# A hybrid attention, Fourier and MLP layer on eight cores: transposed layout, folded DFT, norms applied at evacuation, instruction order computed by list scheduling

## The chip, the cores and the metric

One Trainium2 chip, eight cores, one program on all of them. Each batch entry is shared by two cores: a core owns 1,024 of the 2,048 tokens and computes keys, values and Fourier inputs for all 2,048, so no core talks to another. The metric is the device time of the slowest core in microseconds (us). Some executions fall into a slower state in which the cores of one die show a lower granted clock.

Some words: PSUM is the memory that TensorE writes its sums to, in banks, and an evacuation is the instruction that reads them out; a slot is a buffer for a block of weights; a transfer lands when its data are there; the chain is the work that ended last, followed back from the end of the program to what each step waited for.

## The reference, cut to what matters

```python
h = modulate(rmsnorm(x, g1), sh1, sc1)        # x (4, 2048, 2048); h*(1+scale)+shift
q, k, v, u = split_proj(h @ w_in)             # 1536 | 512 | 512 | 512 columns
q = apply_axial_rope(rmsnorm(heads(q, 12), q_g), tabs)
k = apply_axial_rope(rmsnorm(heads(k, 4), k_g), tabs)
attn = latent_attention(q, k, v, kc, vc)      # keys: 2048 latent + 256 context tokens
four = fourier_mix(u, w_f)                    # Re(2-D DFT over tokens and channels), then a 128x128 map
x = x + gt1 * (concat([attn, four]) @ w_out)
h2 = modulate(rmsnorm(x, g2), sh2, sc2)
x = x + gt2 * (square(relu(h2 @ w1)) @ w2)    # 2048 -> 8192 -> 2048
return rmsnorm(x, final_norm_g)
# the six shifts, scales and gates: silu(c) @ w_ada + b_ada, w_ada being 2048 x 12288
```

All weights come as fp32 and are turned into bf16 by the load.

## The kernel before

Tokens lie on the partitions. x is normalised, transposed 128 by 128 on TensorE, and scale and shift are applied as the transpose is copied out. The modulation comes first, eight blocks, because the shift is needed at that copy:

```python
for j in range(8):
    ada_block(j, 0, 1)                        # shift1 and scale1, 8 x 4.19 MB, all before any norm
...
groups = [(x_oth[0:512, :], 4, 0, 'gs0', 0, [3, 4, 5], 1024, 1024), ...]   # five token groups
...
            for cb in blocks:                 # w_in is fetched again for each of the five groups
                s = wb_next()
                wv = WB[s].rearrange("p (k n) -> p k n", k=16)
                dma('pool', wv, w_in[:, cb * 512:(cb + 1) * 512].rearrange("(k p) n -> p k n", p=128), ...)
                for t in range(ntiles):
                    ...
```

Attention works on halves of a head (512 queries), 24 in all, over 18 chunks of 128 keys. Half of the softmax denominator is summed on TensorE and half on VectorE:

```python
        NPT = 4                               # buffers of exponentials
...
            mm(PS(ob), Vt[:, ch, kh * 128:(kh + 1) * 128], PT[p], ch == 0, ch == 17, ...)
            if ch % 2 == 1:
                mm(PS(ob + 1), ones_bf, PT[p], ch == 1, False, ...)
            elif ch == 0:
                S.add('dve', lambda e, da=da, p=p: e.tensor_copy(out=DACC[da], in_=PT[p]), ...)
            else:
                S.add('dve', lambda e, da=da, p=p: e.tensor_tensor(out=DACC[da], in0=DACC[da], in1=PT[p], op=ALU.add), ...)
...
                S.add('dve', lambda e, rd=rd, ob=ob: e.reciprocal(out=RDEN[rd], in_=PS(ob + 1)), ...)
```

Then come the Fourier groups, 272 matmuls of 512 columns; the output projection, whose weights use the slots of the modulation blocks; a second norm with transposes; sixteen MLP blocks of 256 matmuls; and a final norm, row by row. Each engine runs the order in which the program names the operations.

## Time and profile before

Three executions took 2,193.15 to 2,196.6 us, median 2,195.57.

| of the profiled execution | value |
|---|---|
| busy share: TensorE, VectorE, ScalarE, GpSimd | 83, 43, 29, 18% |
| instructions | 29,071 |
| transposes on TensorE | 584 |
| HBM read | 386.61 MB, of it w_in 84 MB (20 blocks of 4.19 MB) |
| modulation and first norm | 0 to 190 us |
| projections of K, V, U and Q | 190 to 597 us |
| attention | 626 to 1,043 us |
| Fourier, output projection | 1,043 to 1,095, 1,125 to 1,277 us |
| MLP, final norm | 1,277 to 2,163, 2,163 to 2,196 us |

Read 83% as an average over two different programs: an MLP in which TensorE never stops, and 1,277 us before it in which it often does. Only the second can be shortened by order and layout. The lines behind this are shown in the prediction.

### The profile page before, as it was taken

The numbers are of one execution on the slowest core, as the hardware profiler recorded it, in microseconds if no ns is written. First come the engines' busy times: TensorE is split into PE (matmuls) and PEld (weight loads), VectorE is DVE, ScalarE is ACT, GpSimd is POOL, SyncE is SP. The second block draws the span as 40 slices with busy tenths as digits, with TensorE's granted clock in tenths as the row PEclk, the third lists the DMA queues.
The fourth block names the chain that finished last, engine by engine and source line by source line (L and its number), as shares of the span: only waits on it lengthen the run. The fifth ranks groups of instructions, "written<-read, shape, count | busy, mean of one in ns | idle before, by whom it ended". The sixth has DMA issues, their size and how long they took to land.

```text
span 2195.4 us, 29071 instructions; the slowest of 8 cores (2170.3 to 2195.4 us)
## 1 busy us (share of the span) xinstructions
PE 1819.8 (83%) x8352; PEld 821.7 (37%) x8352; DVE 953.2 (43%) x1481; ACT 626.0 (29%) x1211; POOL 387.0 (18%) x221
## 2 busy tenths in 40 slices
PE   2438666868588988877969789999999999999994
PEld 1124323333233333322424334444444444444441
DVE  0025525573655456666023723333333333333346
ACT  0035324321155555565000551111111111111113
POOL 1000000000000000100500330333333333333320
PEclk8659887999889899998989989999999999999997
DMA  9997897868745666500896243444444444444414
GB/s 137 147 195 146 166 155 160 129 112 137 122 77 83 110 103 109 87 1 1 118 236 112 43 77 65 76 76 76 76 75 75 78 75 76 75 76 76 76 31 172
DMA packets 168486, 220.67 MB, mean 101 GB/s; under 512 B 4977, under 2 KB 155636, under 8 KB 163852
## 3 DMA queue, kind: packets, MB, share of 16 engines
q0 software_dynamic: 150032, 176.20, 52.1%
q1 hardware_dynamic: 18300, 42.62, 5.9%
q8 instruction: 71, 1.16, 0.2%
q14 instruction: 83, 0.68, 0.1%
HBM read 386.61 MB, written 8.39 MB: 180 GB/s over the span
## 4 chain that ended last, share of the span: by engine, by line
PE 69%; DVE 11%; DMA 10%; ACT 4%; issue 4%; DVEq 0%; ACTq 0%; POOL 0%; SPq 0%; POOLq 0%
PE psum L286 68%; DMA arena<-w_ada 5%; DVE arena L672 4%; DMA arena<-w_in 3%; DMA arena<-w_out 1%; ACT arena L438 1%; DVE arena L474 1%; DVE arena L466 1%; PE psum L290 1%; DVE arena L478 1%; DVE arena L493 1%; ACT arena L405 1%; ACT arena L872 1%; DVE arena L489 1%; ACT arena L644 1%
## 5 line engine op out<-in xcount | busy, mean ns | idle before, releaser
L286 PE MATMUL psum<-arena 128*128 128x512 bf16 (+1 forms) x7768 | 1776.9, 391 | 254.1 <-DMA arena<-w_ada 78.3
L286 PEld LDWEIGHTS psum<-arena 128*128 128x128 bf16 (+1 forms) x7768 | 776.5, 103 | 1234.1 <-issue 432.7
L841 DVE TENSOR_TENSOR arena<-psum,arena 128x512 f32<-128x512 f32 x512 | 330.0, 686 | 548.6 <-PE psum L286 548.6
L644 ACT ACTIVATE arena<-psum 128x512 bf16<-128x512 f32 x432 | 246.4, 599 | 199.1 <-PE psum L286 93.8
L726 POOL TENSOR_TENSOR arena<-arena 128x2048 bf16<-128x2048 bf16 x64 | 261.9, 4118 | 202.9 <-DMA arena<-w 202.9
L821 ACT ACTIVATE arena<-psum 128x512 f32<-128x512 f32 x128 | 75.4, 589 | 683.6 <-PE psum L286 683.2
L663 DVE TENSOR_TENSOR arena<-arena 128x512 f32<-128x512 f32 x192 | 132.9, 692 | 103.3 <-ACT arena L644 97.8
L290 PE MATMUL psum<-arena 128*128 128x128 bf16 x584 | 55.4, 251 | 89.7 <-DVE arena L415 71.7
L405 ACT ACTIVATE arena<-arena 128x2048 bf16<-128x2048 f32 x26 | 49.8, 1915 | 250.6 <-DMA arena<-x_oth 130.1
L282 POOL DMA_DIRECT2D arena<-w_ada x24 | 27.6, 1150 | 421.7 <-PE psum L286 380.1
L672 DVE RECIPROCAL arena<-psum 128x512 f32<-128x512 f32 x24 | 80.6, 3357 | 41.8 <-PE psum L286 41.8
L282 POOL DMA_DIRECT2D arena<-w_in x20 | 22.8, 1141 | 416.2 <-PE psum L290 218.8
L438 ACT ACTIVATE arena<-psum,arena 128x128 bf16<-128x128 bf16 x208 | 81.6, 473 | 32.9 <-PE psum L290 26.5
L290 PEld LDWEIGHTS psum<-arena 128*128 128x128 bf16 x584 | 46.2, 113 | 107.3 <-issue 98.9
L823 ACT ACTIVATE arena<-arena 128x512 bf16<-128x512 f32 x128 | 80.9, 632 | 11.8
L345 DVE COPY arena<-psum 2x512 f32<-2x512 f32 x24 | 16.3, 677 | 128.2 <-PE psum L286 128.1
L457 DVE CAST arena<-psum 128x512 bf16<-128x512 f32 x29 | 19.7, 690 | 114.7 <-PE psum L286 112.4
L434 DVE TENSOR_SCALAR arena<-psum,arena 128x128 bf16<-128x128 bf16 x208 | 59.7, 339 | 17.6 <-PE psum L290 11.5
L282 POOL DMA_DIRECT2D arena<-w x24 | 25.4, 1059 | 227.8 <-PE psum L286 169.4
L415 DVE TENSOR_SCALAR arena<-arena 128x2048 bf16<-128x2048 f32 x26 | 34.2, 1319 | 43.8 <-ACT arena L410 27.2
L466 DVE TENSOR_REDUCE arena<-arena 128x4 f32<-128x512 f32 x42 | 28.5, 679 | 55.8 <-ACT arena L465 55.8
L760 DVE TENSOR_TENSOR arena<-psum,arena 128x512 f32<-128x512 f32 x32 | 22.1, 690 | 66.9 <-PE psum L286 66.9
(48 smaller groups left out, 404.8 us busy)
## 6 DMA issues: line engine op xcount, KB each, us to landing
arena<-w_ada POOLq DMA_DIRECT2D x24, 2048.0 KB, 15.9
arena<-w POOLq DMA_DIRECT2D x24, 2048.0 KB, 16.0
arena<-w_in POOLq DMA_DIRECT2D x20, 2048.0 KB, 18.1
arena<-x_own SPq DMA_DIRECT2D x16, 1024.0 KB, 10.6
arena<-w POOLq DMA_DIRECT2D x8, 1536.0 KB, 10.3
arena<-x_oth SPq DMA_DIRECT2D x8, 1024.0 KB, 10.8
arena<-w_out POOLq DMA_DIRECT2D x4, 2048.0 KB, 22.2
out<-arena SPq DMA_DIRECT2D x8, 1024.0 KB, 5.4
```

The lines of the kernel that those rows point to most:

```text
L282: return e.dma_start(out=out, in_=in_)
L286: S.add('pe', lambda e, o_=out, l=lhsT, r=rhs, a=start, b=stop: e.matmul(o_, lhsT=l, rhs=r, start=a, stop=b), reads=reads, writes=writes)
L290: S.add('pe', lambda e, o_=out, i_=in_, d_=idt: e.transpose(out=o_, in_=i_, identity=d_), reads=reads, writes=writes)
L405: S.add('act', lambda e, xt=xt, c=c: e.activation(out=cfg['junk'], in_=xt, func=AF.Square, accum_out=stat[:, c:c + 1]), reads=xkeys + list ...
L438: S.add('act', lambda e, o_=o_, i_=i_, sc_=sc_, sh_=sh_: e.activation(out=o_, in_=i_, func=AF.Identity, scale=sc_, bias=sh_), reads=['ps%d ...
L644: S.add('act', lambda e, p=p, sbank=sbank: e.activation(out=PT[p], in_=PS(sbank), func=AF.Exp, scale=SCALE), reads=['ps%d' % sbank, f0], w ...
L663: S.add('dve', lambda e, da=da, p=p: e.tensor_tensor(out=DACC[da], in0=DACC[da], in1=PT[p], op=ALU.add), reads=['pt%d' % p, 'dacc%d' % da] ...
L672: S.add('dve', lambda e, rd=rd, ob=ob: e.reciprocal(out=RDEN[rd], in_=PS(ob + 1)), reads=['ps%d' % (ob + 1), f0], writes=['rden%d' % rd])
L726: S.add('pool', lambda e, s=s, j=j: e.tensor_tensor(out=W2C[s][j], in0=W2C[s][j], in1=GT2, op=ALU.mult), reads=['w2s%d' % s] + ['gt5_%d' % ...
L821: S.add('act', lambda e, r=r, bk=banks[tg]: e.activation(out=RSC[r], in_=PS(bk), func=AF.Relu), reads=['ps%d' % banks[tg], f3], writes=['r ...
L823: S.add('act', lambda e, r=r, bb=bb, j=j, tg=tg: e.activation(out=A2T[bb][:, j, tg * 512:(tg + 1) * 512], in_=RSC[r], func=AF.Square), rea ...
L841: S.add('dve', lambda e, bk=banks[ci], t=t, cb=cb: e.tensor_tensor(out=ACC[t][:, cb * 512:(cb + 1) * 512], in0=PS(bk), in1=ACC[t][:, cb * ...
```

## The change

Intent. Channels lie on the partitions from start to end, since x is handed over transposed, so the transposes of x and of the second norm go. With h = x·(1+scale)·g, the factor 1/rms of a token is applied when the projection leaves PSUM, and the shift becomes a row, shift @ w_in, that is added there. So projections can start when half of the modulation has come, but the K evacuations need the shift rows. Each block of w_in is loaded once. The DFT is folded over the pair of tokens n and 2048−n. The denominator is summed on TensorE with stationaries of 32 columns, four side by side. The order of every engine is computed ahead by list scheduling from modelled durations, with `R.level` as priority, and is then fixed. The diff replaces nearly every line; this is its core, with cuts:

```diff
-        for j in range(8):
-            ada_block(j, 0, 1)
...
+        last = []
+        for i in range(8):
+            last = ada(8 + i, AD0, 'ada', 0.0, 0.0, [7, 6], last)      # scale
+        last = load_win(4, WV, 'wv', 0.1, last)
+        last = load_win(5, WU, 'wu', 0.1, last)
+        last = load_win(3, WK, 'wk', 0.1, last)
+        for i in range(8):
+            last = ada(i, AD0[0:2], 'adz', 0.2, 0.5, [7, 6], last)     # shift, two slots
+        bias_rows(WK, 6, 0.5)
...
+            x = XS[rot('xs', 3)]
+            R.dma('sp', x.rearrange("p k n -> p (k n)"), rows(xt_d, t), 'xs%d' % (n % 3))
...
+        def mb():
+            return 6 + rot('misc', 2)
...
-                mm(PS(ob + 1), ones_bf, PT[p], ch == 1, False, reads=['ones', 'pt%d' % p], writes=['ps%d' % (ob + 1)])
...
+                    R.mms([(PS[5][32 * i:32 * i + 32, :], ones[:, 0:32], pts[c0 + i], c0 == 0, c0 + i + 4 > 17) for i in range(ch - c0 + 1)])
+            R.copy(DHL[0], PS[5])
+            R.tt(DHL[1], PS[5], DHL[0], ALU.subtract)
+            R.mms([(PS[5], selb[0], DHL[0], True, False), (PS[5], selb[0], DHL[1], False, True)])
...
+                stage_b(b, d, tg)
+                if b == NB - 1:
+                    R.level = 5
+                    sq = SQN[rot('sqn', 2)]
+                    R.act(sq, ACC(tg, d), AF.Square)
+                    R.mms([(PS[tg], ones, sq, d == 0, d == 15)])
+                    R.level = 4
```

(The words behind # are added here.)

## The prediction

> **What bounds the kernel now.** I read the page's parts 1, 2 and 4, then the chain in order of time to cut the span into stages, then busy times by stage, then the groups by shape.
>
> ```profile
> span 2195.4 us, 29071 instructions; the slowest of 8 cores (2170.3 to 2195.4 us)
> PE   2438666868588988877969789999999999999994
> PEclk8659887999889899998989989999999999999997
> DMA  9997897868745666500896243444444444444414
> PE 69%; DVE 11%; DMA 10%; ACT 4%; issue 4%; DVEq 0%; ACTq 0%; POOL 0%; SPq 0%; POOLq 0%
> ```
>
> TensorE carries 69% of the chain. It is full from slice 24 on and holed before; the holes, not the full part, are what a rewrite can win. The chain names their edges:
>
> ```profile
> 43.90 23.60 DMA arena<-w_ada
> 74.23 21.51 DMA arena<-w_ada
> ...
> 1095.29 29.72 DMA arena<-w_out
> 1125.15 85.74 PE psum L286 x384
> ...
> 1277.43 886.02 PE psum L286 x4095
> ```
>
> So: w_ada loads to 132 us, a wait for w_out at 1095, the MLP from 1277 to 2163. Busy times in such stretches (columns: stretch, length, busy us with counts for PE, weight load, DVE, ACT, POOL, then clock, DMA share, GB/s):
>
> ```profile
> 0.00:132.00 132.00, 46.35 (x169) 18.60 (x170) 6.22 (x16) 7.51 (x11) 11.23 (x14) 0.76 1.06 152
> 190.00:597.00 407.00, 295.33 (x1521) 140.87 (x1518) 219.65 (x427) 126.12 (x315) 21.69 (x19) 0.90 0.83 144
> 626.00:1043.00 417.00, 345.24 (x1385) 144.52 (x1385) 244.37 (x286) 233.59 (x410) 21.38 (x25) 0.92 0.47 74
> 1043.00:1095.00 52.00, 51.09 (x222) 22.12 (x223) 3.96 (x6) 3.33 (x6) 27.18 (x52) 0.95 0.87 117
> 1125.00:1277.00 152.00, 128.64 (x638) 60.56 (x639) 81.36 (x129) 40.70 (x80) 23.46 (x9) 0.92 0.60 116
> 1500.00:1700.00 200.00, 200.00 (x928) 90.71 (x927) 73.55 (x115) 32.86 (x56) 60.73 (x23) 1.00 0.46 77
> 2163.00:2196.00 33.00, 0.65 (x4) 0.10 (x1) 19.59 (x12) 18.54 (x32) 0.00 (x0) 0.58 0.72 286
> ```
>
> In order: modulation, projections, attention, Fourier, output projection, MLP, final norm. The MLP's 4,096 matmuls take 886.02 us, **216.3 ns each** at clock 1.00: TensorE's own pace, with nothing to hide. I use it as the price of a 512-column matmul. By it the projections' 1,216 matmuls (76 token-tile by weight-block units, 16 each) are worth 263 us; their stage is 407 us long with the DMA at 0.83, since w_in is fetched 20 times. Attention is worth 1,080 x 0.2163 = 234 us plus 256 modulation matmuls, 55 us, but lasts 417. Why, the groups and the VectorE timeline at the seam of two heads show:
>
> ```profile
> L672 DVE RECIPROCAL arena<-psum 128x512 f32<-128x512 f32 x24 | 80.6, 3357 | 41.8 <-PE psum L286 41.8
> 664.00 3.36 DVE L672 RECIPROCAL arena<-psum 128x512 f32<-128x512 f32 x1 [2.21 <-PE psum L286]
> 667.47 0.69 DVE L673 TENSOR_TENSOR arena<-psum,arena 128x512 bf16<-128x512 f32 x1
> 668.07 0.42 DVE L661 CAST arena<-arena 128x512 f32<-128x512 bf16 x1
> ```
>
> VectorE also sums the softmax denominator, so the next head's sums queue behind a 3.36 us reciprocal; they hold the four buffers of exponentials, ScalarE stops, TensorE stops, and the clock falls (0.92 over the stage). That happens 24 times.
>
> **What the Trainium skill says.** (1) "TensorE: Matmul & The Clock Gate", Part 1: an idle array drops to half clock, and three busy cores of a die would trip a limiter to 13/16 clock. The trace agrees on the first (0.76 while loading) and not on the second: all eight cores show 1.00 from 1300 to 2100 us. I therefore keep 216.3 ns. (2) "TensorEngine Tiling (Array Packing)", Theoretical Speedup and Key Properties: 32-column stationaries may run four abreast, but a change of tiling mode drains the array. No instruction of this kernel shows it. (3) "DMA: Bandwidth & Descriptors", Specifications: about 358 GB/s of HBM per core. Here eight w_ada blocks of 4.19 MB in fp32, in 2 KB rows, take 3.5 to 131.9 us, 261 GB/s; a w2 block in 8 KB rows, issued in two parts, lands 12.8 us after issue, 328 GB/s. The page's figure is a ceiling that longer rows approach.
>
> **The change part by part.**
>
> *Start.* Before, all of scale and shift (33.5 MB) lands before any norm. After, x arrives transposed, only the scale half (16.8 MB) is needed for x*(1+scale)*g, the shift becomes a row added after projection, and 1/rms is applied at PSUM evacuation. Rows are 16 KB long, so I take 335 GB/s (estimate from 328). First projection: 16.8 + 4.2 (V weights) + 3.1 (three x tiles) MB = 24.1 MB, 72 us, **about 75 us** instead of 190. 416 of the 584 transposes (55.4 us / 584 = 95 ns each, 40 us) go; 288 one-column matmuls for the sums of squares come, 16 per tile, at about 0.08 us (estimate below a transpose's 95 ns): 23 us.
>
> *Projections of K, V, U.* Weights loaded once. 832 x 0.2163 = 180 us. But the context tiles' V and all later K evacuations need the shift rows, last in the queue: 16.8 + 12.6 + 16.8 + about 13 MB of x and rope = 59 MB / 335 = 177 us, plus 8 us of chain. I count what can run by 185 us: eight tiles of V, U, K and five units more, 464 of 832 matmuls; then the banks of the two context tiles are held and TensorE waits. Left: 368 x 0.2163 = 80 us, plus 20 for sums, bias rows and transposes: stage ends at **285**.
>
> *First Q block and Fourier.* 128 matmuls, 28 us. Folding n with 2048-n and sharing cosine and sine sums between mirrored outputs leaves 22 matmuls of 512 per group, 88 instead of 272: 19 us, plus 8 for small ones: **to 340**. The tables come in while projections run.
>
> *Attention.* Per head half: 36 x 0.2163 = 7.79 us, denominator on TensorE as 18 matmuls with 32 columns four abreast at about 0.07 (a third of 216.3, estimate) = 1.3, broadcast 0.43: 9.5 us; x 24 = 228. Beside it: two Q blocks 256 x 0.2163 = 55; 32 modulation blocks of 16 tiled matmuls and 8 tiny ones, about 1.6 each, 51; transposes and bias 10. Sum 344 us of TensorE. ScalarE: 432 x 0.599 = 259 + 16 x 1.3 for Q norms = 280. VectorE: 24 x 6 (reciprocal 3.36 and four of 0.6 to 0.7) + 16 x 4.6 + 32 x 1.2 = 256. Both lie beside it, and with 14 buffers of exponentials and sums no longer on VectorE the reciprocal leaves the loop. I add 5% for seams: 361, **to 701**, against 417 + 52 before with no Q in it.
>
> *Output projection.* w_out is preloaded into the freed h and Q buffers, so the 30 us wait goes. 512 + 32 for sums of squares = 544 x 0.2163 = 118, plus 5; the transposes and four-step norm at its end (152 us before) go. **To 824.**
>
> *MLP.* Same 4,096 matmuls: 886. POOL's gate multiplication (64 x 4.1 us) goes but was off the path. VectorE's evacuation stays one pass of about 0.69 us per 0.865 us of TensorE. 32 matmuls more in the last block, 7. **To 1717.**
>
> *Tail.* ScalarE's full passes over rows go, being summed during the last block; 2 + 16 x 0.69 + leftovers of the first half + about 3 for the store: 22 instead of 33. **1739**, and 16 us for the seams between stages, whose order was fixed ahead from modelled durations: **1755 us**, ratio 0.80.
>
> Check: TensorE's work after the first projection, 180 + 36 + 55 + 344 + 118 + 893 = 1,626 us, plus 75 and 22, is 1,723; no good schedule beats that by much.
>
> **Rivals.**
> 1. *The tiled matmuls do not overlap.* Denominators then cost 18 x 0.216 = 3.9 us, 24 x 2.6 = 62 more, and modulation blocks some 20 to 30: about 1,840. For: the mode changes ten times per head half. Against: nothing but the page's multiple.
> 2. *Attention becomes bound by the single denominator bank.* Copy, subtract, broadcast, reciprocal hold bank 5 for some 6 us per half of 14; if the order misplaces the next half's sums, TensorE waits 2 to 3 us: 24 x 2.5 = 60, about 1,815. Against: Q and modulation work lies between.
> 3. *DMA binds longer.* Attention's stage moves 67 MB of w_ada, 17 of w_out and more in 361 us, over 240 GB/s[...]. At 261 GB/s the start alone slips by 40: 1,795.
> 4. *The gain is hidden anyway.* Against: the MLP is untouched at 886, but the other 1,309 us hold barely 800 of TensorE work.
> 5. *A denser program trips a lower clock.* At 13/16 it would cost some 350 us. Against: the MLP is already dense at 1.00.
> 6. *Better than thought:* overlap of stages removes my 5% and the seams: 1,715.
>
> **Range and chances.** Rivals 1 to 3 are partial and each would add 40 to 85; best case 1,715. So 1,700 to 1,840 holds 8 in 10. To be within 2% of before, over 390 us of my 440 would have to vanish: faster 0.97, same 0.02, slower 0.01.
>
> **What would show it.** First long run of matmuls near 75 us, and a hole before about 185; one w_in load per block; no reciprocal in the chain and clock near 1.00 in attention; attention near 360 us with TensorE over 0.9 busy; four tiled matmuls in about one's time; no wait on w_out; MLP within 1% of 886. Wrong would be: attention with ScalarE waits at every half, a start past 100 us, or an MLP slower than 216 ns per matmul.

## The result, and the profile after

Before, in the same rounds: 2,193.15, 2,195.57 and 2,196.6 us, and one slow execution. After: 1,842.05, 1,842.44 and 1,844.09 us, and one slow execution of 2,091.07 us in which one die had a clock of about 0.83. The ratio is 0.8391, interval 0.8377 to 0.8405: about 353 us shorter. Ratios are the mean time of one kernel's runs over that of the other's of the same rounds, so they are not quite the ratio of the medians. Executions over 1.5% slower than the fastest of the same kernel are left out of the means. Results are correct. The prediction was 1,755 us; 1,843 lies 3 us above its range.

The page of the profiled execution after, the same lines as shown of before:

```profile
span 1840.5 us, 24669 instructions; the slowest of 8 cores (1829.4 to 1840.5 us)
PE   0379879979997999999999999999999999999994
PEclk9989989979998999999999999999999999999996
DMA  9995623336466669940742345543345543245205
PE 77%; DMA 10%; DVE 7%; issue 4%; ACT 2%; DVEq 0%; SPq 0%; POOL 0%; ACTq 0%; POOLq 0%
```

TensorE's share of the chain rose from 69 to 77%, and its row, counted from slice 0, is 9 from slice 9 on but for slice 12 and the last. The holes that remain are nearly all in the first nine slices, before 414 us, and at the very end. HBM read fell from 386.61 to 314.61 MB and transposes from 584 to 168.

The chain in order of time (start, length, what):

```profile
90.87 24.95 DMA xs_85<-xt
...
713.82 3.37 DVE rd_143 L804
...
796.67 1004.93 PE ps L102 x4660
```

Loads of x stand in the early chain (this one, and another of 26.17 us from 118.34), and a reciprocal of 3.37 us in the attention (one of six that stand in this chain at full length, beside four of under 1 us; none was to be there), and from 797 to 1,801.6 us a single run of matmuls: output projection and MLP without one break. Busy times by stretch, in the columns of the prediction (PE, weight load, DVE, ACT, POOL, then clock, DMA share, and GB/s as landed, where a weight counts in bf16, half of what was read):

```profile
76.00:148.00 72.00, 49.53 (x257) 20.88 (x258) 20.63 (x26) 14.70 (x18) 1.05 (x2) 0.92 1.01 221
148.00:228.00 80.00, 72.17 (x528) 32.42 (x526) 24.39 (x49) 19.71 (x29) 2.11 (x4) 0.94 0.56 128
228.00:337.00 109.00, 96.65 (x592) 45.69 (x588) 86.66 (x144) 40.37 (x92) 30.00 (x28) 0.92 0.32 77
337.00:419.00 82.00, 66.24 (x353) 30.44 (x353) 47.99 (x91) 20.39 (x48) 15.88 (x15) 0.88 0.28 58
419.00:797.00 378.00, 348.69 (x2299) 125.28 (x2300) 237.10 (x345) 236.80 (x477) 32.66 (x48) 0.98 0.73 135
797.00:1801.60 1004.60, 1004.60 (x4657) 454.86 (x4655) 434.26 (x582) 204.74 (x330) 16.89 (x32) 1.00 0.38 71
1801.60:1841.00 39.40, 15.70 (x31) 3.08 (x30) 21.92 (x33) 19.25 (x34) 0.00 (x0) 0.56 0.58 213
```

In the first row TensorE works 49.53 of 72 us beside full DMA; in the second the DMA share has fallen to 0.56 although the modulation is not complete; in the third VectorE, too, is busy 86.66 of 109 us. Attention has TensorE at 0.92 of the time and a clock of 0.98 (0.83 and 0.92 before). Output projection and MLP are full. The tail is 39 us.

Stage by stage, where the prediction puts it and where the trace has it:

| stage | predicted length, us | measured, us | difference |
|---|---|---|---|
| first V projection starts | 75 | 76.0 | +1 |
| K, V, U (to the last K matmul, 336.9) | 210 | 260.9 | +51 |
| Q block 0 and Fourier (to 416.5) | 55 | 79.6 | +25 |
| attention (to 799.9) | 361 | 383.4 | +22 |
| output projection and MLP (to 1,801.6) | 1,016 | 1,001.7 | −14 |
| tail (to 1,840.5) | 22 | 38.9 | +17 |
| seams | 16 | in the stages | −16 |
| sum | 1,755 | 1,840.5 | +86 (rounded) |

**Reading the K, V, U stage.** The shift half of the modulation goes through two slots, and its issuer, GpSimd, waits for TensorE to free them. GpSimd's timeline at the issue of the fifth shift block, and where the shift row has come (in brackets, how long the engine had been idle and what released it):

```profile
173.38 0.53 POOL L161 DMA_DIRECT2D wada_79<-w_ada  x1 [30.58 <-PE ps L102]
```

```profile
228.02 1.26 POOL L138 TENSOR_TENSOR y_90<-y_90,bk 128x512 f32<-128x512 f32 x1 [21.82 <-DVE bk L154]
```

GpSimd's longest wait there, 73.6 us, is not yet a matter of order: the first two shift blocks stood in the queue behind the weights of V, U and K, landed at about 132 and 141 us, and were used at once. After these two, the shift blocks were issued at 133.02, 142.27, 173.38, 178.93, 187.86 and 205.67 us: a slot is free only when the block's matmuls have run, and in TensorE's fixed order those stand behind tiles whose x came late. The third block landed at 147.5 us, 14.5 after its issue, but its matmuls ran at 172.20; the fourth landed at about 153.5 and was used at 177.76. On the path to the last block, waits of this kind add up to about 33 us (24 for the fourth block, 8 for the sixth). So the row BK, predicted for 185 us, was there at 228. Meanwhile x came slowly: from 76 to 148 us its queue landed 7.34 MB in 1,008 packets, and the queue of the weights 8.54 MB in 1,171 packets. That is 7.34 + 2 × 8.54 = 24.4 MB read, 339 GB/s, so the rate was what I had assumed; but x got only 0.30 of it, about one tile per 10 us.

**Reading the attention.** TensorE's timeline at one group of denominator sums, with the full matmuls around it (start, length, operation):

```profile
641.75 0.38 PE L102 MATMUL ps<-pt_130,v 128*128 128x512 bf16 x1
642.06 0.39 PE L102 MATMUL ps<-pt_127,cb 128*32 128x512 bf16 x1
642.06 0.39 PE L102 MATMUL ps<-pt_128,cb 128*32 128x512 bf16 x1
642.07 0.39 PE L102 MATMUL ps<-pt_129,cb 128*32 128x512 bf16 x1
642.07 0.39 PE L102 MATMUL ps<-pt_130,cb 128*32 128x512 bf16 x1
642.39 0.39 PE L102 MATMUL ps<-qT,kT 128*128 128x512 bf16 x1
```

Four 32-column matmuls start within 0.01 us: they do run four abreast. But they start 0.31 us after the full matmul before them, and the next full one 0.32 us after them, where full ones follow each other by 0.22. So each way of the change costs about 0.1 us, and the group takes 0.42 us out of the run of full matmuls. Over the whole attention such groups, alone or two in a row, take about 2.0 us per half (the waits left out), and the broadcast 0.43: about 2.4 us, where 1.73 was predicted.

**Reading the tail.** ScalarE's first square of the last block, and VectorE's first final multiplication:

```profile
1801.68 0.63 ACT L133 ACTIVATE sqn_155<-acc_149 128x512 bf16<-128x512 f32 x1 [24.63 <-PE ps L102]
```

```profile
1814.53 5.39 DVE L141 SCALAR_TENSOR_TENSOR acc_149<-acc_149,cf,tn_169 128x512 f32<-128x512 f32 x8 [12.30 <-ACT tn_169 L133]
```

The last MLP matmul ends at 1,801.6; ScalarE, idle for 24.63 us, only then starts the squares. All 32 come after the MLP, and the multiplications wait for their sum.

### The profile page after: what moved, and what is told of

Read it like the earlier page. It is cut to its first block, busy times and chain, and to the rows that moved or that the text cites. A ratio compares the mean times of both kernels' runs of the same rounds, so it can differ in the third digit from the quotient of the medians.

```text
span 1840.5 us, 24669 instructions; the slowest of 8 cores (1829.4 to 1840.5 us)
## 1 busy us (share of the span) xinstructions
PE 1665.4 (90%) x8916; PEld 719.7 (39%) x8916; DVE 890.1 (48%) x1309; ACT 565.4 (31%) x1038; POOL 109.9 (6%) x153
## 3 DMA queue, kind: packets, MB, share of 16 engines
HBM read 314.61 MB, written 8.39 MB: 175 GB/s over the span
## 4 chain that ended last, share of the span: by engine, by line
PE 77%; DMA 10%; DVE 7%; issue 4%; ACT 2%; DVEq 0%; SPq 0%; POOL 0%; ACTq 0%; POOLq 0%
PE ps L102 76%; DMA xs_85<-xt 4%; DMA xs_87<-xt 3%; DMA wada_82<-w_ada 1%; DMA wadb_84<-w_ada 1%; DVE rd_143 L804 1%; DMA wq_71<-w_in 1%; DMA xs_86<-xt 1%; DVE acc_151 L141 1%; DMA wq_72<-w_in 1%; PE ps L114 1%; DVE rd_144 L804 0%; DVE t_0_98 L138 0%; DVE t_1_99 L138 0%; DVE qst L615 0%
## 5 line engine op out<-in xcount | busy, mean ns | idle before, releaser
L141 DVE SCALAR_TENSOR_TENSOR acc_151<-ps,modcol,acc_151 128x512 f32<-128x512 f32 x272 | 204.4, 751 | 270.5 <-PE ps L102 248.6
L102 PE MATMUL ps<-a_0_163,w_0_161 128*128 128x512 bf16 x1024 | 231.5, 379 | 0.0
L102 PE MATMUL ps<-a_1_164,w_1_162 128*128 128x512 bf16 x1024 | 230.3, 379 | 0.0
L141 DVE SCALAR_TENSOR_TENSOR acc_149<-ps,modcol,acc_149 128x512 f32<-128x512 f32 x136 | 101.4, 751 | 145.6 <-PE ps L102 136.5
L141 DVE SCALAR_TENSOR_TENSOR acc_150<-ps,modcol,acc_150 128x512 f32<-128x512 f32 x136 | 102.2, 751 | 141.3 <-PE ps L102 130.3
L102 PE MATMUL ps<-qT,kT 128*128 128x512 bf16 x432 | 153.2, 384 | 1.8 <-DVE qT L154 0.9
L102 PEld LDWEIGHTS ps<-a_0_163,w_0_161 128*128 128x128 bf16 x1024 | 100.2, 98 | 120.8
L102 PEld LDWEIGHTS ps<-a_1_164,w_1_162 128*128 128x128 bf16 x1024 | 100.2, 98 | 120.9
L102 PE MATMUL ps<-h_0_152,w_1_160 128*128 128x512 bf16 x512 | 115.7, 379 | 0.0
L102 PE MATMUL ps<-h_0_152,w_0_159 128*128 128x512 bf16 x512 | 115.4, 379 | 0.0
L102 PE MATMUL ps<-h_2_154,w_0_159 128*128 128x512 bf16 x384 | 88.1, 379 | 0.0
L102 PE MATMUL ps<-h_2_154,w_1_160 128*128 128x512 bf16 x384 | 88.1, 379 | 0.0
L102 PEld LDWEIGHTS ps<-h_0_152,w_0_159 128*128 128x128 bf16 x512 | 50.1, 98 | 60.4
L102 PEld LDWEIGHTS ps<-h_0_152,w_1_160 128*128 128x128 bf16 x512 | 50.0, 98 | 60.5
L133 ACT ACTIVATE rs_168<-ps 128x512 f32<-128x512 f32 x32 | 19.1, 596 | 169.8 <-PE ps L102 169.8
L133 ACT ACTIVATE rs_167<-ps 128x512 f32<-128x512 f32 x32 | 19.1, 597 | 167.7 <-PE ps L102 167.6
L133 ACT ACTIVATE rs_166<-ps 128x512 f32<-128x512 f32 x32 | 19.1, 596 | 167.6 <-PE ps L102 167.6
L133 ACT ACTIVATE rs_165<-ps 128x512 f32<-128x512 f32 x32 | 19.1, 596 | 165.8 <-PE ps L102 165.8
L102 PEld LDWEIGHTS ps<-h_2_154,w_0_159 128*128 128x128 bf16 x384 | 37.6, 98 | 45.2
L102 PEld LDWEIGHTS ps<-h_2_154,w_1_160 128*128 128x128 bf16 x384 | 37.6, 98 | 45.2
L102 PEld LDWEIGHTS ps<-qT,kT 128*128 128x128 bf16 x432 | 40.7, 97 | 34.0 <-issue 16.4
L804 DVE RECIPROCAL rd_143<-ps 128x512 f32<-128x512 f32 x12 | 40.3, 3357 | 5.4 <-PE ps L102 5.1
```

The lines of the kernel that those rows point to most:

```text
L102: ins = e.matmul(o, lhsT=l, rhs=r, start=a, stop=b)
L133: self.add('act', lambda e: e.activation(out=out, in_=in_, func=func, scale=scale, **kw), reads, writes, dur, level=level)
L141: self.add('dve', lambda e: e.scalar_tensor_tensor(out=out, in0=a, scalar=s, in1=b, op0=op0, op1=op1), [a, b] + ([] if isinstance(s, float ...
L804: R.add('dve', lambda e, o_=rd, i_=PS[5]: e.reciprocal(out=o_, in_=i_), [PS[5]], [rd], 3.36)
```

## The experiments

Each kernel is the one after with the edit shown, unless it says otherwise. The gain over after is the difference of two ratios to the kernel before, times about 2,197 us. Runs 1 to 4, 5 to 8 and 9 to 12 each shared their runs of the kernel before, the first four on one chip and the rest on another; for runs 1 to 8 the ratio of after is the 0.8391 of its first comparison, for 10 to 12 the 0.8392 of run 9. "Last K matmul" and the like are given for all cores, or as their mean; in after the last K matmul ends at 331 to 339 us, mean 334.7 (core 3, shown above, is a late one), and attention, here from the last matmul of the Fourier transforms to the first of the output projection, takes 381 us in the mean. Every edit also makes the list scheduling compute another order for the whole program; run 6 shows what that alone can do to a stage.

Against the gains expected: runs 5, 8, 9 and 10 came out inside the range, 11 inside by its median, 1, 2, 3 and 7 up to 3 us short of it, 4 and 12 further short, and 6 where its rival put it.

**1. Squares in the order of need.**

```diff
                 if b == NB - 1:
-                    R.level = 5
+                    R.level = 4
```

> The changed kernel, but the squares and row sums of the last MLP block keep the priority of that block instead of a lower one, so that the list scheduler may put them between its matmuls. Theory (the tail was mis-sized because all 32 squares run after the last MLP matmul: ScalarE idle 24.6 us before the first of them, then one every 0.6 to 0.7 us): the tail after the last MLP matmul falls from 39 to 20 to 24 us, TensorE's last block grows by at most 7 us, and the whole is 10 to 17 us shorter, 1826 to 1833 us. Rival (the tail is set by VectorE's 32 final multiplications and the stores, whatever the squares do): under 4 us.

Correct, median 1,834.68 us, ratio 0.8347 (0.8328 to 0.8366): 0.0044 × 2,197 = 9.7 us shorter. From the last MLP matmul to the end it now takes 20.6 us instead of 38.9; some of the won time went into the last block, where about 7 us of sums now lie (32 x 0.2163). VectorE's last entry in its timeline shows what bounds the rest:

```profile
1812.35 16.64 DVE L141 SCALAR_TENSOR_TENSOR acc<-acc,cf,tn 128x512 f32<-128x512 f32 x25
```

25 of the 32 multiplications still lie after the MLP. So the place of the squares was the cause of the long tail, and VectorE's 0.67 us per multiplication is its new bound.

**2. No shift rows (wrong).** The five shift rows and columns are set to zero.

```diff
-        bias_rows(WK, 6, 0.5)
-        bias_bc(selb[0], 7, BK)
...
+        for z in (BK, BKC, BVD, bvc, buc):
+            R.memset(z, 0.0)
```

> WRONG RESULT ON PURPOSE: the shift rows that K, V and U get after their projection are set to zero at the start instead of being computed, so no evacuation waits for the second half of w_ada, which is loaded all the same. Theory A (the stage of K, V and U is 52 us longer than predicted because the shift rows come at 228 us instead of 185 and K's normalisation piles up on VectorE behind them): the last K matmul moves from 337 us to 295 to 310, and the whole is 25 to 40 us shorter. Theory B (most of it is lost before, when TensorE waits for x tiles that come slowly beside the weights): under 12 us, and the holes in TensorE between 76 and 148 us stay.

Wrong (relative error 0.257), 1,823.96 us, ratio 0.8290 (0.8272 to 0.8308): 22 us shorter. The last K matmul comes at 309 to 320 us, 312.3 in the mean instead of 334.7, so the shift rows are worth about 22 of the 51 us. Some 5 us of this are the matmuls that make the rows (in after, three groups of 1.05 us or more and the broadcasts), which this edit drops as well. The hole from 76 to 148 stays (TensorE 50 to 55 of 72 us on the first four cores), so it has another cause: each theory was right in part.

**3. Banks of its own for the Fourier part.**

```diff
-        for _ in q_block(0, [0, 1, 2, 3, 4], [6, 7]):
+        for _ in q_block(0, [0, 1, 2], [6, 7]):
...
         def mb():
-            return 6 + rot('misc', 2)
+            return 3 + rot('misc', 3)
```

> The Fourier part takes PSUM banks 3, 4 and 5 in place of 6 and 7, and the first Q block takes its projections in banks 0 to 2 only, so that Fourier need not wait for the Q block's transposes, which use 6 and 7. Theory (the stretch from 337 to 419 us was 82 us instead of 55 because Fourier, ready since its tables landed, could not fill TensorE while VectorE worked off the Q block's normalisation): first Fourier matmul before 360 us instead of 383, the hole around 370 to 386 closes, 10 to 20 us shorter in all. Rival (VectorE's normalisation of Q sets the start of attention anyway, and Fourier then only moves): under 4 us.

Correct, 1,835.66 us, ratio 0.8350 (0.8335 to 0.8365): 9 us shorter. The matmuls of the Fourier transforms start at 367 to 376 us instead of 383 to 392, but the last of them comes only 6 us sooner in the mean: VectorE is still busy with the Q norms until about 384 us (32.14 of 34 us from 350), and the copies that Fourier needs stand behind them. From the last K matmul to that point it takes 68.5 us instead of 77.8. Attention ends at 768 to 780, 19 us sooner in the mean, so it is itself 12 us shorter, which was not expected. About half of the 19 is given back at once. The waits of one core from 770 to 830 us show it:

```profile
PE ps L102 <- DVE acc L141: 6.0, 1, 6.0
DVE acc L141 <- DMA acc<-xo: 4.8, 1, 4.8
```

The output projection now comes before its residual x has landed, since that buffer is held by the last modulation blocks. From its first matmul to the end it takes 1,052 us instead of 1,041.5. A gain in one stage ran into a load that the old timing had hidden.

**4. The reciprocal on ScalarE.**

```diff
-            R.add('dve', lambda e, o_=rd, i_=PS[5]: e.reciprocal(out=o_, in_=i_), [PS[5]], [rd], 3.36)
+            R.act(rd, PS[5], AF.Ln)
+            R.act(rd, rd, AF.Exp, scale=-1.0)
```

> The softmax reciprocal as a logarithm and an exponential on ScalarE (2 x about 0.6 us) in place of VectorE's 3.36 us. My rival 2 (the single denominator bank, held through copy, subtract, broadcast and reciprocal, stops TensorE at the seams; the chain has nine reciprocals of 3.37 us in attention): 9 x 2 to 3, so 12 to 25 us shorter. If attention is bound by TensorE's own work with the seams hidden: between 3 us shorter and, for 24 x 1.2 = 29 us more of ScalarE, 8 us longer.

Correct, 1,838.7 us, ratio 0.8360 (0.8345 to 0.8375): 6.8 us shorter, less than expected (and the chain had six full reciprocals, not the nine that the expectation counts). Attention takes 371 us instead of 381 in the mean. That is in keeping with a reciprocal that holds up some seams, not all 24; but run 6 moves this stage by 7 us by order alone, so it is not shown for more than a part.

**5. x in bf16 on the queue of the weights, in order of need, six buffers.**

```diff
-        XS = [at('xs_%d' % i, 144 + 8 * i, [16, 128]) for i in range(3)]
+        XS = [at('xs_%d' % i, 144 + 4 * i, [16, 128], BF16) for i in range(6)]
...
-            R.dma('sp', x.rearrange("p k n -> p (k n)"), rows(xt_d, t), 'xs%d' % (n % 3))
+            R.dma('pool', x.rearrange("p k n -> p (k n)"), rows(xt_d, t), 'xs%d' % (n % 6), level=0.09 if n < 8 else 0.2,
+                  after=wl[min(n // 2, 3)])
```

> The changed kernel with x loaded on the weights' own queue, cast to bf16 by the load, into six buffers instead of three, in the order of need (two tiles after the scale half, two after the V weights, two after the U weights, two after the K weights, then before the shift half). In the changed kernel x tiles and weights run on two queues, and between 74 and 148 us seven x tiles got about a third of the traffic, one per 10 us, where the order of instructions counted on half. Theory (x comes late, TensorE starves 22 us before 148 us, and the matmuls of the shift half wait behind tiles that wait for x): last K matmul from 337 to 310 to 325 us, whole 10 to 25 us shorter. Rival (the bytes bind, not their order: the DMA share is 1.0 to 148 us, so what x gains the weights lose): within 5 us either way.

Correct, 1,835.25 us with one slow execution of four, ratio 0.8340 (0.8306 to 0.8374): 11 us shorter. Two stretches of this kernel:

```profile
76.00:148.00 72.00, 64.51 (x371) 29.17 (x370) 26.57 (x34) 22.25 (x29) 4.22 (x8) 0.95 1.03 170
220.00:240.00 20.00, 8.34 (x40) 3.81 (x41) 20.00 (x38) 6.87 (x18) 11.06 (x8) 0.52 0.13 34
```

The hole is mended (64.51 busy instead of 49.53), the shift rows come at 206 to 209 us instead of 220 to 228, but the last K matmul comes only 8 us sooner in the mean. The second line says why: the eight waiting K tiles are released at once, VectorE is busy 20.00 of 20 us with their norms, and TensorE, waiting for it, has 8.34 us of work. A pile-up takes the place of the wait. Queue, buffers and order were changed together; which of them mends the hole is not separated.

**6. The order computed with another transfer model.**

```diff
-DMA_RATE = 340e3
+DMA_RATE = 315e3
...
-                both = min(max(dma_free[other] - start, 0.0), 2 * need)
-                dma_free[e] = start + need + both / 2
+                share = 1 / 3. if e == 'sp' else 2 / 3.
+                both = min(max(dma_free[other] - start, 0.0), need / share)
+                dma_free[e] = start + need + both * (1 - share)
```

> Only the constants by which the program orders its instructions are changed: DMA at 315 GB/s in all instead of 340, with the x queue getting a third beside the weights' queue instead of half, as the trace of the changed kernel shows between 74 and 148 us. The same instructions in another order. Theory (the order was fixed from a too kind picture of the DMA, so TensorE's queue stands behind late tiles and the shift half is delayed): shift rows ready before 215 us instead of 227, whole 5 to 20 us shorter. Rival (the order hardly matters, since whatever is put first something else comes later): within 4 us.

Correct, 1,842.31 us, ratio 0.8376 (0.8358 to 0.8394): 3 us, and the intervals overlap. The shift rows come at 216 to 222, some 6 us sooner, the last K matmul at 336 to 342, no sooner, and attention takes 374 us instead of 381. So these constants alone are not the cause, and a mere change of order can shift a stage by 5 to 7 us. The 315 GB/s in it, which I had from landing times, is too low: counting packets gives 339 in this stretch. The share of a third is right.

**7. Denominator sums with full matmuls.**

```diff
-                    R.mms([(PS[5][32 * i:32 * i + 32, :], ones[:, 0:32], pts[c0 + i], c0 == 0, c0 + i + 4 > 17) for i in range(ch - c0 + 1)])
-            R.copy(DHL[0], PS[5])
-            R.tt(DHL[1], PS[5], DHL[0], ALU.subtract)
-            R.mms([(PS[5], selb[0], DHL[0], True, False), (PS[5], selb[0], DHL[1], False, True)])
+                    R.mms([(PS[5], ones, pts[c0 + i], c0 + i == 0, c0 + i == 17) for i in range(ch - c0 + 1)])
```

> The softmax denominators as 18 full matmuls with a 128-column stationary of ones per head half, which already broadcast the sum, in place of 18 tiled ones four abreast plus copy, subtract and broadcast. By the trace a tiled group of four takes 0.22 us to the next tiled group and 0.33 us to a full matmul, so tiled sums and broadcast cost about 2.0 us per half and full ones 18 x 0.216 = 3.9: 24 x 1.9 = 45 us longer, 35 to 55 (my prediction said 24 x 2.2 = 52 between the two). Rival (the seams, where copy, subtract and broadcast stood, close, and TensorE had room): under 25 us longer.

Correct, 1,876.67 us, ratio 0.8539 (0.8504 to 0.8573): 32.5 us longer. Attention takes 416 us instead of 381, which is 35 / 24 = 1.45 us per half. Eighteen full matmuls are 18 × 0.2163 = 3.89 us, so the tiled form with its broadcast costs about 3.89 − 1.45 = 2.4 us per half, if TensorE bounds both. The count in the trace of after gives the same. I had put it at 1.73.

**8. The kernel before, with the whole denominator on TensorE.** This tests the reading of before.

```diff
-            if ch % 2 == 1:
-                mm(PS(ob + 1), ones_bf, PT[p], ch == 1, False, reads=['ones', 'pt%d' % p], writes=['ps%d' % (ob + 1)])
-            elif ch == 0:
...
-            if ch == 17:
-                mm(PS(ob + 1), ones_f, DACC[da], False, True, reads=['onesf', 'dacc%d' % da], writes=['ps%d' % (ob + 1)])
+            mm(PS(ob + 1), ones_bf, PT[p], ch == 0, ch == 17, reads=['ones', 'pt%d' % p], writes=['ps%d' % (ob + 1)])
```

> The kernel before with one part of the change alone: all denominator sums on TensorE (18 bf16 matmuls with ones per head half) in place of half of them on VectorE; the reciprocal stays on VectorE. It adds 24 x 9 x 0.216 = 47 us of matmuls and takes away 25 us of fp32 ones. My reading of the kernel before (VectorE's sums queue behind the 3.36 us reciprocal and hold the exponentials' buffers, so TensorE stops 24 times): attention from 417 to 340 to 380 us, the whole 30 to 70 us shorter than before. Rival (the seams are set by something else, as ScalarE or the modulation blocks): 0 to 25 us longer than before.

Correct, 2,149.59 us, ratio 0.9764 (0.9732 to 0.9796) to the kernel before: about 52 us shorter. On core 1 the exponentials run from 605.3 to 1,036.4 us before and from 598.3 to 975.7 here, 431 against 377 us. That stretch of this run, same columns as above:

```profile
598.30:975.70 377.40, 361.15 (x1627) 161.58 (x1625) 112.57 (x81) 256.70 (x431) 22.36 (x26) 0.98 0.54 83
```

VectorE is busy 113 us, where it was 252 in the same stretch of before, and TensorE 0.96 of the time instead of 0.84, at a clock of 0.98 instead of 0.92. In before, the exponentials on core 1 stood idle for VectorE's sums for 97.9 us in all (80 waits); here for none. The edit also takes away the fp32 matmuls that closed VectorE's half of each sum, 24.7 us in before, and adds 47 us of bf16 ones, so TensorE got more work, not less. So VectorE's sums behind its reciprocal did hold attention up, as the prediction read it.

**9. After, unchanged, as control.**

> The changed kernel unaltered, on the chip of the next three runs, so that they can be compared with it directly. Expected as before: 0.839 of the time of the kernel before, within 0.003.

Median 1,844.75 us with one slow execution of six, ratio 0.8392 (0.8362 to 0.8422): the first result again.

**10. Runs 2 and 5 together (wrong).**

> WRONG RESULT ON PURPOSE: shift rows set to zero and x on the weights' queue in one. Apart they gave 22 us (last K matmul from about 336 to 311) and 11 us (to 328; there TensorE was 15 us busier before 148 us and the shift rows came 19 us sooner, but VectorE was then full from 207 to 245 us with K normalisations that had all waited for them, and TensorE idled 26 us there). Theory (the two causes lie in series: x holds up the start, the shift rows pile K's normalisation up): together the last K matmul comes at 282 to 297 us, near the 285 of my prediction, and the whole is 35 to 50 us shorter than the changed kernel. Rival (a third thing, such as VectorE's total work in the stage, holds it): last K matmul after 303 us, the whole 22 to 32 us shorter.

Ratio 0.8222 (0.8145 to 0.8299), 37 us shorter. The four executions are of two kinds: 1,795.32 and 1,796.83, and 1,817.24 and 1,817.86. In the profiled one, of the second kind, six cores have their last K matmul at 290 us and spans of 1,790 to 1,795 us; cores 0 and 1 have it at 313 and take 1,813 and 1,815. Core 0 and core 2 of it:

```profile
148.00:190.00 42.00, 42.00 (x254) 18.08 (x253) 25.26 (x37) 12.65 (x22) 9.29 (x9) 0.81 0.89 147
```

```profile
148.00:190.00 42.00, 40.99 (x310) 19.62 (x314) 30.12 (x46) 13.76 (x24) 11.81 (x10) 1.00 1.03 170
```

Both are full, but core 0 has a clock of 0.81 and does 254 matmuls where core 2 does 310. Without that, the last K matmul is at 290 us, 44.5 us sooner than in the mean of after (46 against core 3): of the 51 us that the stage was over, some 45 are gone. The two executions without it, at 1,796 us, are about 48 us below the median of the control; the 37 above mixes both kinds. Alone, the two edits brought 22 and 8. They stand in series: take the shift rows away and tiles still wait for x; bring x early and they wait for the shift rows, then for VectorE.

**11. Three correct mends together:** runs 1, 3 and 4, and the modulation blocks brought forward, against what run 3 met.

```diff
-                while na < 48 and (na - 16) * 24 < 32 * (u + 1):
+                while na < 48 and (na - 16) * 20 < 32 * (u + 1):
```

> A version meant to be better: squares in order (10 us alone), Fourier on its own banks (9 us alone, where attention ended 17 to 20 us sooner but TensorE then waited 6 us for the residual, whose buffer the last modulation blocks held), reciprocal on ScalarE (7 us alone), and the modulation blocks paced to be done by head half 20 instead of 24, which frees that buffer. If they add up: 10 + 15 + 7 = 32 us shorter than the changed kernel, 1806 to 1818 us. Rival (two of them close the same seams of attention): 18 to 24 us shorter.

Correct, six executions of 1,813.77 to 1,821.91 us, median 1,815.91, ratio 0.8267 (0.8237 to 0.8297): 27 us shorter than the control, a little more than the three gains alone (9.7 + 9 + 6.8 = 25.5).

**12. Run 11 and the x of run 5.**

> The same with x on the weights' queue in bf16 as well (11 us alone). If it adds up: 40 to 45 us shorter than the changed kernel, 1796 to 1806 us; result correct, as x is rounded to bf16 for the projections only and the residual stays fp32. Rival (VectorE, full after the shift rows, gives nothing back and Fourier's earlier start collides with it): as the version without it, within 4 us.

Correct, six executions of 1,807.87 to 1,822.12 us, median 1,809.64, ratio 0.8256 (0.8208 to 0.8304): 30 us shorter than the control by ratio, 35 by the medians. It has the lowest median of all correct kernels here. The part with x brought about 6 us by the medians instead of the 11 alone; the intervals of 11 and 12 overlap. In two of its executions, at 1,822 us, cores 0 and 1 again have a lower mean clock, 0.97 against 0.98, and are the longest.

## Why the prediction was right or wrong

**Right: the reading of before.** The prediction said that attention was held up by VectorE, not by TensorE or ScalarE. Run 8 takes VectorE's sums away, though TensorE gets more to do, and wins 52 us. Of TensorE's own work in that stage the prediction left out 24.7 us of fp32 matmuls; that does not change the reading.

**Right: the start.** First projection predicted at 75 us, measured 76.0; and the rate of 335 GB/s holds (339 from 76 to 148 us).

**Right: output projection and MLP,** at 216 ns per matmul, clock 1.00, no wait for w_out. The stage came 14 us shorter than put; half of that are the 32 sums of the last block (7 us), which were priced here and ran in the tail. The 16 us set apart for seams appear in no row of their own; what the seams cost is in the longer stages. These two offsets, 30 us, hide part of what went wrong elsewhere.

**Wrong by 51 us: "Projections of K, V, U".** The failed step is "the shift rows, last in the queue: ... 59 MB / 335 = 177 us, plus 8 us of chain". It took the transfers for one queue that is never stopped. By 148 us the plan held: 18.53 × 2 + 11.00 = 48.1 MB had been read in 144.5 us, 333 GB/s (the queues' bytes, as above). Then the DMA share fell to 0.56, because the shift blocks had two slots and these came free only as TensorE, in its fixed order, got to them (33 us of waiting on the path to the last block); TensorE had waited for x, which had 0.30 of the bytes. The rows came at 228, not 185. Runs 2, 5 and 10 show that the late rows and the late x are both causes and stand in series; run 10, without them, ends the stage at 290 us, and I had put 285. That the two slots pass the lateness of x on to the rows is read from the trace; no run gave the shift blocks more slots. In run 5 a third part showed that I had not priced at all: the norms of the K tiles, held back together, fill VectorE when they are let go. Rival 3, the DMA binding longer, was near to this, but put it at the start and in attention, and as a lack of bandwidth.

**Wrong by 25 us: "First Q block and Fourier".** The step "19 us, plus 8 for small ones: to 340" takes TensorE's work for the length of the stretch, the Fourier matmuls filling it while the Q norms run. They could not start, for their PSUM banks, 6 and 7, are those of the Q block's transposes. Run 3 gives them others: they start 16 us sooner, but the stretch is only 9 us shorter. VectorE's norms of this Q block, 8 × 4.6 = 37 us by the prediction's own price, were not set against the stretch: VectorE is busy 33.99 of 36.5 us from 350 to 386.5, and in run 3 Fourier waits behind it. That is read from the traces; no run takes it away, and the other 16 us are not separated further.

**Wrong by 22 us: "Attention".** Two terms. The denominator at "18 matmuls ... at about 0.07 = 1.3, broadcast 0.43" was mis-sized: 2.4 us per half instead of 1.73, by run 7 and by the count in the trace, × 24 = 16 to 17 us. Four abreast was right; the changes of mode, into and out of five groups in each half, were not priced. And "the reciprocal leaves the loop" was at most partly so: it stands in the chain, and run 4 wins 7 us by moving it, though part of that may be its other order. That is rival 2, one denominator bank, at a fraction of the 60 us it was given. That 17 and 7 cover the excess is partly luck: the modulation blocks, put at 1.6 us each, take about 0.8 in the trace, some 25 us less for 32, so some 20 us, waits among them, are not accounted for; and run 3, made for the stage before, shortens attention by 12 us, and run 6 by 7 through its order. Rival 1, no overlap of tiled matmuls, fell: four start within 0.01 us.

**Wrong by 17 us: "Tail".** The step "full passes over rows go, being summed during the last block" was wrong. The sums were written beside the last block, but with priority 5 against its 4, and list scheduling put all 32 squares after it. Run 1 changes that one figure and the tail is 20.6 us, where I had put 22. The whole gained only 9.7, since the sums now take time in the last block.

**Direction and size.** Faster, as given 0.97. Of the 440 us that I promised, 353 came. The prediction's closing check, 1,723 us, holds a term of 36 us that it derives nowhere. Three of the four wrong steps have one form: I priced the work of a stage and added little for its order, because the order was computed. A computed order is only as good as the priorities, slots and banks that it is given.

**What stays open:** 5 to 10 of the 51 us in the K stage (run 10 against my 285, and it drops the 5 us of making the rows); 16 us of the Fourier stretch; which waits of attention a better order would close; and why a pair of cores now and then gets a clock of 0.81.

## What to carry to other kernels

When a load's slot is freed by an engine with a fixed order, the load is part of that order: check what each slot waits for before counting bytes over bandwidth. In a list-scheduled kernel, read every shared PSUM bank and every priority as a dependency, for a late priority moves work behind the critical path as surely as a wait. And expect mends to be worth less or more together than alone, for waits in series hide each other, and a stage that ends early may meet a load that isn't there yet.

## What the Trainium skill lacked or had wrong

- "TensorE: Matmul & The Clock Gate", Part 1, has the peak-current limiter take the whole die to 13/16 once three of its cores run dense matmuls. Here all eight cores ran the MLP densely at 1.00 in the profiled execution, a fast one (from 1,300 to 1,800 us, TensorE busy 495 us or more of 500); one die fell to about 0.83 on average in one execution in four of the first comparison; and in run 10 two cores of a die alone had 0.81 from about 112 to 228 us while the others had 0.96 to 1.00. A clock near 13/16 exists, but neither always nor for a whole die.
- "TensorEngine Tiling (Array Packing)", Key Properties, says that a change of tiling mode drains the engine, with no figure. Here a tiled group starts 0.31 us after the full matmul before it, and the full matmul after it 0.32 us later, instead of 0.22, so about 0.1 us each way; all in all the tiled sums cost about 2.4 us per half of 18, where I had reckoned 1.73 with a third of a full matmul's time for each.
- "DMA: Bandwidth & Descriptors", Queues, rings and completion order, states that an engine takes packets from its queues in turn, but not what follows for a load that converts fp32 to bf16. Here the two queues' packets were nearly equal in number (1,008 and 1,171 from 76 to 148 us) and in landed size (7.3 KB), so the unconverted x had 0.30 of the bytes read.
- No page gives the duration of a reciprocal of 128x512 fp32 on VectorE, here 3,357 ns, or of that engine's scalar_tensor_tensor with one tensor in PSUM and a scalar per partition, here 751 ns (the tensor_tensor in its place in the kernel before took 686). The longer one made no difference here, being under the 865 ns that TensorE needs for the four matmuls before it.
